# One pool of raw weight tiles for both halves of the MLP, and the first pair's weight forms written earlier

## The chip, the cores and the metric

The kernel runs on one core of a Trainium2 chip. The metric is device time in microseconds (us) for one execution. All engines of the core run their own instruction streams: TensorE (PE, matmuls and transposes, with PEld for its weight loads), VectorE (DVE), ScalarE (ACT), GpSimd (POOL) and SyncE (SP, which here only issues DMAs). They wait for each other on semaphores, and each stream is in order: an instruction that waits holds everything behind it on its engine, and a DMA that waits to be issued holds every later DMA of that queue.

## The reference, cut to what matters

Two layers, 256 tokens of width 2048, float32. Each layer is a mixer (attention and a short gated convolution, both fed by one projection) and an MLP. Cut:

```python
for l in range(DEPTH):                       # 2
    h = _rmsnorm(x, attn_norm_g[l])
    proj = h @ w_in[l]                       # 2048 -> 6144: q, k, v, gate_b, gate_c, conv_in
    attn = differential attention over q, k, v (8 heads), normalised
    conv = gate_b * _short_conv(gate_c * conv_in, conv_w[l])
    x = x + jnp.concatenate([attn, conv], axis=-1) @ w_out[l]
    hm = _rmsnorm(x, mlp_norm_g[l]) @ w_up[l]                  # 2048 -> 8192
    x = x + jnp.square(jax.nn.relu(hm)) @ w_down[l]            # 8192 -> 2048
return x
```

The weights are 2 x (2048 x 6144 + 2048 x 2048 + 2 x 2048 x 8192) float32 numbers, 403 MB, each read once.

## The kernel before

**Numbers in two parts.** TensorE multiplies in a rounded float32 format. Each weight tile is therefore cast to a rounded part (`hi`, on ACT) and a remainder (`lo = raw - hi`, on DVE), and a product is three matmuls (hi x hi, hi x lo, lo x hi; for some products the two activation parts stand side by side, so that two matmuls do). A weight tile of 0.5 MB (128 partitions x 1024 numbers) costs one ACT cast, one DVE subtraction, and then some matmuls. The cast tiles come from a pool `wpool` with three buffers for `hi` and three for `lo`.

**Jobs.** Class `Weights` (L265) holds a list of jobs. `take()` (L310) hands out the next cast tile and sees to it that the casts of the next three jobs (`AHEAD`) are written into the program. A job loads a raw tile by a DMA on SP's queue and casts it in `halves` (L274), or in `column` (L683) for the up weights.

**The mixer** (L599) runs q, k, v for two groups of heads, then the projections gc and ci of the convolution four times (attention of the second group runs between their matmuls), then gb, and last the output projection `o` in four column chunks (`linear`, L325). Its pools, in the order in which they are opened, with their size in each partition: biasp 16 KB, tmp 12 KB (attention's temporaries), rpool 16 KB (four raw tiles of 4 KB), bpool 64 KB (eight tiles of 8 KB: among them the four `cat` tiles that are the input of `o`).

**The MLP** (L667) is made of two passes. In the first, for each of 32 pairs `i` of 128-wide hidden columns, the up projection of the pair is made (`up_part`, L779: two columns c, each in two halves kh of the 2048 inputs), evicted (`evict`, L797), squared with ReLU (`square`, L802, which also writes the activations to DRAM, `hid`, by a DMA on POOL's queue) and, `LAG` = 2 pairs later, multiplied into the left half of the output with a Strassen-like scheme of seven products (`product`, L826). These products need the down weights of pair `i` in several forms, made by `quarters(i)` (L706): b1, b2 straight from the raw tile `draw` (1 MB), t13 and t24 from sums of its quarters, each again as hi and lo. Three jobs make them: `plain` (b1, b2), `sums` (the differences t, and t13) and `more` (t24). For the first pair their ACT and DVE instructions are marked `keep`, that is held in the order in which they are written (`late`, L118). The last two pairs are multiplied without the scheme (L910 to L920, the jobs of `rows`, L741).

In the second pass (L937 to L962) the activations are read back from DRAM (`block`, L884: a load `back` of 0.5 MB and its split into g) and multiplied with the right half of the down weights, one job per 0.5 MB (`weights.straight`, L770), in blocks (b, n) of two jobs each.

**Pools of the MLP.** Opened in this order: fpool 20 KB, dpool 16 KB (two `draw` tiles), and then in a scope `first` spool 40 KB (the weight forms) and upool 24 KB (three raw up tiles `uraw` of 8 KB). `first` is closed after the first pass, and rpool (four raw tiles of 4 KB) and gpool 32 KB are opened in its place. Pools lie on a stack, so a tile of a new pool stands where tiles of the closed pools stood. Its first write waits for the last reader of whatever overlaps it. Mixer and MLP both start at the same address, which gives, in KB of each partition:

```
          0       16     28      44      60      76      92   100  108
mixer     [ biasp  |tmp   |rpool |bpool  0 |  1 |  2 |  3 |  4 |  5 |  6 |  7 ]
MLP, 1st  [ fpool 0-20 | dpool 20-36 | spool 36-76 | upool 76-100 ]
MLP, 2nd  [ fpool 0-20 | dpool 20-36 | rpool 36-52 | gpool 52-84  ]
```

**What sets the order.** PE's instructions run in the order in which they are written. ACT, DVE, POOL and SP are ordered at build time by a scheduler, which places an instruction where its own model thinks it becomes ready, with what is written earlier first. So where a tile lies decides when its load may start, and by that where the load stands in SP's queue.

Of the kernel before, what the change touches and what calls it, by code (L numbers as in the profile page):

```python
# [9 lines left out]
F32 = mybir.dt.float32  # L10
# [5 lines left out]
P = 128  # L16
# [12 lines left out]
CH = 512  # L29
WC = 256  # L30
KG = 4
RAW = 4
# [69 lines left out]
def trunk(ctx: ExitStack, tc: tile.TileContext, x, w_in, w_out, conv_w, q_norm_g, k_norm_g,  # L102
          lambda_q1, lambda_k1, lambda_q2, lambda_k2, subln_g, attn_norm_g, mlp_norm_g,
          w_up, w_down, rel_bias, selector, out):
    nc = tc.nc
# [159 lines left out]
    class Weights:  # L265
# [22 lines left out]
        def plain(self, w, row, c, nk):  # L288

            cols = 2 * CH // nk  # L290

            def make():
                raw = self.early.pop(0) if self.early else load()
                return self.halves(raw)

            def load():
                raw = self.pool.tile([P, nk, cols], F32, tag="raw", name="raw", bufs=RAW)
                nc.sync.dma_start(
                    raw, w[row:row + nk * P, c:c + cols].rearrange("(k p) c -> p k c", p=P))
                return raw  # L300

            make.load = load
            self.jobs.append(make)
# [363 lines left out]
    def mlp(l, mnorm, last):  # L667

        norm = None if last else Norm(0, l + 1)
        mT = mnorm.tiles  # L670
        with ExitStack() as scope:
            fpool = scope.enter_context(tc.tile_pool(name="fpool", bufs=2))
            dpool = scope.enter_context(tc.tile_pool(name="dpool", bufs=2))
            first = scope.enter_context(ExitStack())
            spool = first.enter_context(tc.tile_pool(name="spool", bufs=1))
            upool = first.enter_context(tc.tile_pool(name="upool", bufs=3))
            work.start(mnorm.factors(), 1)


            weights = Weights(None)  # L680
            raws, forms = {}, {}

            def column(i, c, kh):  # L683
# [15 lines left out]
            def load_rows(i, col):  # L699
                raw = dpool.tile([P, 2, 2 * CH], F32, tag="draw", name="draw")  # L700
                nc.sync.dma_start(
                    raw, w_down[l][i * 2 * P:(i + 1) * 2 * P, col:col + 2 * CH].rearrange(
                        "(k p) c -> p k c", p=P))
                return raw

            def quarters(i):  # L706


                keep = late if i == 0 else lambda ins: None

                def parts(src, tag, bufs):
                    hi = spool.tile(list(src.shape), F32R, tag=f"{tag}h", name=f"{tag}h", bufs=bufs)
                    lo = spool.tile(list(src.shape), F32R, tag=f"{tag}l", name=f"{tag}l", bufs=bufs)
                    keep(nc.scalar.activation(hi, src, AF.Copy))  # L714
                    keep(nc.vector.tensor_sub(lo, src, hi.bitcast(F32)))
                    return hi, lo

                def plain():
                    raw = forms["raw"] = load_rows(i, 0).rearrange("p k (n c) -> p k n c", n=2)
                    h1, l1 = parts(raw[:, 0, 0], "b1", 2)  # L720
                    h2, l2 = parts(raw[:, 1], "b2", 1)
                    return (h1, l1), (h2[:, 0], l2[:, 0]), (h2[:, 1], l2[:, 1])

                def sums():
                    raw = forms["raw"]
                    t = forms["t"] = spool.tile([P, 4, CH], F32, tag="t", name="t")

                    keep(nc.vector.tensor_sub(t[:, 0:2], raw[:, :, 1], raw[:, 0]))
                    h, lw = parts(t[:, 0:2], "t13", 1)

                    keep(nc.vector.tensor_add(t[:, 2], t[:, 1], raw[:, 0, 0]))
                    keep(nc.vector.tensor_sub(t[:, 3], raw[:, 1, 0], t[:, 2]))
                    return (h[:, 0], lw[:, 0]), (h[:, 1], lw[:, 1])

                def more():
                    h, lw = parts(forms["t"][:, 2:4], "t24", 1)
                    return (h[:, 0], lw[:, 0]), (h[:, 1], lw[:, 1])

                return plain, sums, more

            def rows(i, k, box):  # L741
# [19 lines left out]
            for i in range(NP - LAG, NP):  # L761
                box = []
# [3 lines left out]


            order = [(b - n, n) for b in range(NB2 + 1) for n in range(2) if 0 <= b - n < NB2]
            for b, n in order:
                weights.straight(w_down[l], b * KG * P, KG, (2 + n) * CH)  # L770


            hid = [dram.tile([P, KG * S], F32, name=f"hid{l}{b}") for b in range(NB2)]
# [23 lines left out]
            def evict(acc, dst):  # L797
                ev = nat.tile([P, 2, S], F32, tag="wide", name="ev")
                nc.scalar.activation(ev, acc, AF.Copy)
                nc.vector.tensor_add(dst.rearrange("p a c -> p (a c)"), ev[:, 0], ev[:, 1])  # L800

            def square(i, h):  # L802


                u = h[:, 0:4].rearrange("p a c -> p (a c)")
                nc.scalar.activation(u, u, AF.Relu)
                top = h[:, 0:4].rearrange("p (k t) c -> p k t c", t=2)[:, :, 0]
                nc.vector.tensor_mul(top, top,
                                     mnorm.ratio.unsqueeze(1).to_broadcast([P, 2, P]))
                nc.scalar.activation(u, u, AF.Square)  # L810
                nc.gpsimd.dma_start(hid[i // 2][:, i % 2 * 2 * S:(i % 2 + 1) * 2 * S], u)  # L811
                n = 4
                if i < NP - LAG:
                    n = 8
                    nc.vector.tensor_add(h[:, S1], h[:, A21], h[:, A22])
                    nc.vector.tensor_sub(h[:, S2], h[:, S1], h[:, A11])
                    nc.vector.tensor_sub(h[:, S3], h[:, A11], h[:, A21])
                    nc.vector.tensor_sub(h[:, S4], h[:, A12], h[:, S2])
                f = fpool.tile([P, 2, 8, P], F32R, tag="f", name="f")
                nc.scalar.activation(f[:, 0, :n], h[:, :n], AF.Copy)  # L820
                nc.vector.tensor_sub(f[:, 1, :n], h[:, :n], f[:, 0, :n].bitcast(F32))
                return f
# [10 lines left out]
            for i in range(NP):  # L833
                j = i - LAG
                end = i == NP - 1
                h = fpool.tile([P, 8, P], F32, tag="h", name="h", bufs=1)
                if i == 0:
                    two = mm.tile([P, 2, CH], F32, tag="mm2", name="up0")
                    two = [two[:, c].rearrange("p (h s) -> p h s", h=2) for c in range(2)]
                    for kh in range(2):  # L840
                        for c in range(2):
                            up_part(two[c], kh)
                            if kh:
                                evict(two[c], h[:, 2 * c:2 * c + 2])
                    fs[0] = square(0, h)
                    continue
                for c in range(2):
                    if i < LAG:
                        acc = bank("upw").rearrange("p (h s) -> p h s", h=2)
                    else:  # L850
                        acc = column_bank()
                    up_part(acc, 0)
                    up_part(acc, 1)
                    evict(acc, h[:, 2 * c:2 * c + 2])
                    if c == 1:
                        fs[i] = square(i, h)
                    if j == 0 and c == 0:
                        for pair in ((1, 6), (2, 3)):
                            w2 = mm.tile([P, 2, CH], F32, tag="mm2", name=f"pr{l}{pair[0]}")
                            prods[pair[0]], prods[pair[1]] = w2[:, 0], w2[:, 1]  # L860
                        for n in (4, 5, 7):
                            prods[n] = bank(f"pr{l}{n}")
                    if j >= 0 and c == 0:
                        b11, b21, b22 = weights.take()
                        t1, t3 = weights.take()
                        product(1, j, A11, b11, end)
                        product(2, j, A12, b21)
                        product(3, j, S4, b22)
                        product(5, j, S1, t1, end)
                        work.tick()  # L870
                    elif j >= 0:
                        t2, t4 = weights.take()
                        product(7, j, S3, t3, end)
                        product(6, j, S2, t2, end)
                        product(4, j, A22, t4)
                        work.tick()


            first.close()
            rpool = scope.enter_context(tc.tile_pool(name="rpool", bufs=RAW))  # L880
            gpool = scope.enter_context(tc.tile_pool(name="gpool", bufs=3))
            weights.pool = rpool

            def block(b):  # L884

# [25 lines left out]
            for j in range(NP - LAG, NP):  # L911
                for k in range(2):
                    b = weights.take()
# [94 lines left out]
```

## Time and profile before

| | |
|---|---|
| median of 3 runs | 2210.66 us (2209.38 to 2211.1) |
| the profiled execution's own time | 2213.11 us, of which the span from first to last instruction is 2211.3 us |
| granted TensorE clock, mean | 0.991 |
| PE busy | 2163.5 us (98%), 11066 matmuls and transposes |
| DVE / ACT / POOL busy | 1610.7 / 1286.7 / 137.8 us |
| read from HBM | 425.84 MB, 201 GB/s over the span |
| one cast of 128x1024 | ACT 1055 ns (L282), DVE 1227 ns (L283) |
| one matmul of 512 columns | starts every 227 ns at full clock |
| loads: `uraw` 1 MB, `draw` 1 MB, `raw` of w_down 0.5 MB, `back` 0.5 MB | 5.7, 5.1, 4.5, 5.3 us from issue to landing (medians) |

How to read it: where an instruction has waited, a row of the timeline ends in the idle time before it and in what ended it. Matmuls are pipelined, so the rows give a matmul of 512 columns about 390 ns while the next one starts 227 ns after it; time lost is read from the starts. PE's granted clock is a share of full speed. The trace names a tile by its name in the program: `uraw`, `uhi`, `ulo` are an up weight tile raw and in its two parts; `draw` is the raw tile of a pair's down weights; `raw`, `whi`, `wlo` are those of all other weights.

### The profile page before, as it was taken

The numbers are of one execution on the slowest core, as the hardware profiler recorded it, in microseconds if no ns is written. First come the engines' busy times: TensorE is split into PE (matmuls) and PEld (weight loads), VectorE is DVE, ScalarE is ACT, GpSimd is POOL, SyncE is SP. The second block draws the span as 40 slices with busy tenths as digits, with TensorE's granted clock in tenths as the row PEclk, the third lists the DMA queues.
The fourth block names the chain that finished last, engine by engine and source line by source line (L and its number), as shares of the span: only waits on it lengthen the run. The fifth ranks groups of instructions, "written<-read, shape, count | busy, mean of one in ns | idle before, by whom it ended". The sixth has DMA issues, their size and how long they took to land.

```text
span 2211.3 us, 29293 instructions
## 1 busy us (share of the span) xinstructions
PE 2163.5 (98%) x11066; PEld 1835.1 (83%) x11066; DVE 1610.7 (73%) x2229; ACT 1286.7 (58%) x1718; POOL 137.8 (6%) x194
## 2 busy tenths in 40 slices
PE   8999999889999999999999999996999999999999
PEld 7888888678888888888888888885888888888887
DVE  6677655589898989755566776555989898987554
ACT  6456445466666666654455654444666666665443
POOL 2021100000000000100011111000000000001000
PEclk9999999999999999999999999998999999999999
DMA  7654666666666666477575546656676666665775
GB/s 260 181 153 153 188 184 180 193 210 207 220 213 214 218 210 217 169 243 242 186 247 174 160 152 189 183 160 211 208 223 208 219 214 213 218 210 198 251 239 161
DMA packets 293518, 446.65 MB, mean 202 GB/s; under 512 B 11427, under 2 KB 192245, under 8 KB 293376
## 3 DMA queue, kind: packets, MB, share of 16 engines
q1 hardware_dynamic: 286672, 423.66, 61.5%
q0 software_dynamic: 6656, 21.10, 2.5%
q8 instruction: 86, 1.41, 0.3%
q14 instruction: 56, 0.46, 0.1%
q10 hardware_dynamic: 48, 0.02, 0.0%
HBM read 425.84 MB, written 18.90 MB: 201 GB/s over the span
## 4 chain that ended last, share of the span: by engine, by line
PE 94%; issue 4%; DMA 1%; DVE 0%; POOL 0%; ACT 0%; SPq 0%; DVEq 0%; POOLq 0%
PE upc L789 30%; PE dn L950 16%; PE pr L829 13%; PE o L338 8%; PE q L338 4%; PE gc L360 4%; PE ci L360 4%; PE gb L360 4%; PE v L338 4%; PE k L338 4%; PE sc L500 1%; PE av L536 1%; DMA hid<-h 1%; DMA raw<-in_w_down_dram 1%; PE tpn L402 1%
## 5 line engine op out<-in xcount | busy, mean ns | idle before, releaser
L283 DVE TENSOR_TENSOR wlo<-raw,whi 128x1024 fp32r<-128x1024 f32 (+1 forms) x386 | 473.4, 1227 | 384.2 <-ACT whi L282 382.8
L282 ACT ACTIVATE whi<-raw 128x1024 fp32r<-128x1024 f32 (+1 forms) x386 | 407.2, 1055 | 481.1 <-PE dn L950 163.6
L789 PE MATMUL upc<-nT,uhi 128*128 128x512 f32 x1920 | 480.2, 392 | 0.0
L694 ACT ACTIVATE uhi<-uraw 128x1024 fp32r<-128x1024 f32 x256 | 270.4, 1057 | 308.2 <-PE upc L789 274.4
L789 PEld LDWEIGHTS upc<-nT,uhi 128*128 128x128 f32 x1920 | 354.9, 189 | 69.0
L695 DVE TENSOR_TENSOR ulo<-uraw,uhi 128x1024 fp32r<-128x1024 f32 x256 | 312.6, 1222 | 121.3 <-ACT uhi L694 118.7
L950 PE MATMUL dn<-whi,g 128*128 128x512 f32 x1024 | 316.3, 389 | 0.0
L789 PEld LDWEIGHTS upc<-nT,ulo 128*128 128x128 f32 x1920 | 262.8, 191 | 18.8
L789 PE MATMUL upc<-nT,ulo 128*128 128x256 f32 x1920 | 268.5, 283 | 0.0
L950 PEld LDWEIGHTS dn<-whi,g 128*128 128x128 f32 x1024 | 192.2, 188 | 40.0
L950 PE MATMUL dn<-wlo,g 128*128 128x512 f32 x512 | 199.2, 389 | 0.0
L338 PE MATMUL o<-whi,cat 128*128 128x512 f32 x512 | 159.6, 390 | 0.0
L338 PEld LDWEIGHTS o<-whi,cat 128*128 128x128 f32 x512 | 96.2, 188 | 19.7
L950 PEld LDWEIGHTS dn<-wlo,g 128*128 128x128 f32 x512 | 96.1, 188 | 19.8
L829 PE MATMUL pr<-t13h,f 128*128 128x512 f32 x240 | 95.1, 396 | 11.5 <-ACT t13h L714 11.5
L338 PE MATMUL o<-wlo,cat 128*128 128x512 f32 x256 | 99.7, 389 | 0.0
L811 POOL DMA_DIRECT2D hid<-h x64 | 34.9, 545 | 982.8 <-ACT h L810 982.8
L338 PE MATMUL q<-whi,nT 128*128 128x512 f32 x256 | 85.7, 404 | 2.7 <-ACT nT L248 2.7
L338 PE MATMUL k<-whi,nT 128*128 128x512 f32 x256 | 85.3, 399 | 0.0
L829 PE MATMUL pr<-t24h,f 128*128 128x512 f32 x240 | 84.0, 390 | 0.0
L829 PE MATMUL pr<-b2h,f 128*128 128x512 f32 x240 | 84.0, 390 | 0.0
L338 PE MATMUL v<-whi,nT 128*128 128x512 f32 x256 | 83.4, 396 | 0.0
(330 smaller groups left out, 3443.5 us busy)
## 6 DMA issues: line engine op xcount, KB each, us to landing
uraw<-in_w_up_dram SPq DMA_DIRECT2D x128, 1024.0 KB, 5.7
raw<-in_w_in_dram SPq DMA_DIRECT2D x192, 512.0 KB, 3.9
draw<-in_w_down_dram SPq DMA_DIRECT2D x64, 1024.0 KB, 5.1
raw<-in_w_down_dram SPq DMA_DIRECT2D x128, 512.0 KB, 4.5
raw<-in_w_out_dram SPq DMA_DIRECT2D x64, 512.0 KB, 3.7
hid<-h POOLq DMA_DIRECT2D x64, 256.0 KB, 3.5
back<-hid SPq DMA_DIRECT2D x32, 512.0 KB, 5.3
rev<-by_dist_d POOLq DMA_DIRECT2D x4, 1024.0 KB, 11.2
```

What stands on the lines that cost most here:

```text
L282: nc.scalar.activation(hi[:, k], raw[:, k], AF.Copy)
L283: nc.vector.tensor_sub(lo[:, k], raw[:, k], hi[:, k].bitcast(F32))
L338: nc.tensor.matmul(acc[:, t], a.ap[:, pa, k % KG, t * P:(t + 1) * P], (hi, lo)[pw][:, j], start=(k == 0 and n == 0), stop=(k == nk - 1 and ...
L360: nc.tensor.matmul(acc[:, f, 0] if part else acc[:, f], wt[:, k % 4, fs], a.ap[:, 0, k % KG] if part else a.ap[:, :, k % KG], start=(part ...
L402: nc.tensor.transpose(tp[:, i * S + t * P:i * S + (t + 1) * P], xs[n][:, t, k * P:(k + 1) * P], ident)
L500: nc.tensor.matmul(sc[:, :W], qT[m * DK:(m + 1) * DK, a, i, t * P:(t + 1) * P], kT[m * DK:(m + 1) * DK, b, i, :W], start=(n == 0), stop=(n ...
L694: nc.scalar.activation(hi, src, AF.Copy)
L695: nc.vector.tensor_sub(lo, src, hi.bitcast(F32))
L789: nc.tensor.matmul(acc[:, 0] if part else acc, wt[:, k], a.ap[:, 0, k % KG] if part else a.ap[:, :, k % KG], start=(part == 0 and kh == 0 ...
L811: nc.gpsimd.dma_start(hid[i // 2][:, i % 2 * 2 * S:(i % 2 + 1) * 2 * S], u)
L829: nc.tensor.matmul(prods[n], fs[j][:, pa, a], b[pw], start=(j == 0 and m == 0), stop=(stop and m == 2))
L950: nc.tensor.matmul(acc[:, t], f[:, pa, k, t * P:(t + 1) * P], (hi, lo)[pw][:, k % 2], start=(b == 0 and k == 0 and m == 0), stop=(b == NB2 ...
```

## The change

It does three things.

1. `upool` becomes the first pool that the MLP opens, and stays open through both passes. The stack of the MLP is then:

```
          0            24        44      60               92   100
MLP, 1st  [ upool 0-24 | fpool 24-44 | dpool 44-60 | spool 60-100 ]
MLP, 2nd  [ upool 0-24 | fpool 24-44 | dpool 44-60 | gpool 60-92 ]
```

2. The second pass has no raw pool of its own. A new helper `four` loads the 1 MB of a block (b, n) with one DMA into a tile of `upool` (same tag `uraw`, so the same three buffers as the up weights) and makes two jobs of it, one per half.

3. For the first pair, `quarters(0)` returns jobs that only hand out forms already made. They are made by `forms["begin"]()`, which is called behind `square(0, h)`: the `draw` load, b1, b2, t and t13 of the first pair are written into the program behind the first pair's up columns, and no longer when the jobs in the list are reached (with the last half column of the second pair and the first of the third). t24 stays where it was.

```diff
         with ExitStack() as scope:
+            upool = scope.enter_context(tc.tile_pool(name="upool", bufs=3))
             fpool = scope.enter_context(tc.tile_pool(name="fpool", bufs=2))
             dpool = scope.enter_context(tc.tile_pool(name="dpool", bufs=2))
             first = scope.enter_context(ExitStack())
             spool = first.enter_context(tc.tile_pool(name="spool", bufs=1))
-            upool = first.enter_context(tc.tile_pool(name="upool", bufs=3))
             work.start(mnorm.factors(), 1)
-            weights = Weights(None)
+            weights = Weights(upool)
...
+                if i == 0:
+                    made = {}
+                    begin = lambda: made.update(p=plain(), s=sums())
+                    forms["begin"] = begin
+                    return lambda: made["p"], lambda: made["s"], more
                 return plain, sums, more
...
             order = [(b - n, n) for b in range(NB2 + 1) for n in range(2) if 0 <= b - n < NB2]
+
+            def four(b, n, k, box):
+                def make():
+                    if k == 0:
+                        raw = upool.tile([P, KG, CH], F32, tag="uraw", name="raw")
+                        nc.sync.dma_start(
+                            raw, w_down[l][b * KG * P:(b + 1) * KG * P,
+                                           (2 + n) * CH:(3 + n) * CH].rearrange(
+                                               "(k p) c -> p k c", p=P))
+                        box.append(raw)
+                    return weights.halves(box[0][:, k:k + 2])
+                weights.jobs.append(make)
+
             for b, n in order:
-                weights.straight(w_down[l], b * KG * P, KG, (2 + n) * CH)
+                box = []
+                four(b, n, 0, box)
+                four(b, n, 2, box)
...
                     fs[0] = square(0, h)
+                    forms["begin"]()
                     continue
...
             first.close()
-            rpool = scope.enter_context(tc.tile_pool(name="rpool", bufs=RAW))
             gpool = scope.enter_context(tc.tile_pool(name="gpool", bufs=3))
-            weights.pool = rpool
```

## The prediction

> **What bounds the kernel now.** First the page's busy times: PE is busy for 2163.5 of 2211.3 us, DVE for 73%, ACT for 58%, so only what makes PE wait, or run slowly, counts. Next PE's list of waits (what waited on what: us in total, times, longest):
>
> ```profile
> PE up L789 <- ACT uhi L694: 18.5, 2, 9.6
> PE pr L829 <- ACT t13h L714: 11.5, 2, 5.8
> PE pr L829 <- DVE t13l L715: 3.1, 2, 2.0
> PE pr L916 <- DVE wlo L283: 1.5, 2, 0.8
> PE up L789 <- ACT ev L799: 1.4, 2, 0.7
> ```
>
> Each stands there twice, once per layer, and all lie around the MLP. The first: TensorE has finished `o` and the first up weights are not cast. Then PE's timeline of layer 0 (start, duration, what, idle before):
>
> ```profile
> 398.03 0.39 PE L338 MATMUL o<-whi,cat 128*128 128x512 f32 x1
> 407.39 3.78 PE L789 MATMUL up<-nT,uhi 128*128 128x512 f32 x8 [8.98 <-ACT uhi L694]
> ...
> 423.11 2.00 PE L789 MATMUL upw<-nT,uhi 128*128 128x512 f32 x8
> ...
> 425.91 2.00 PE L789 MATMUL upw<-nT,uhi 128*128 128x512 f32 x8
> ...
> 447.87 0.79 PE L829 MATMUL pr<-t13h,f 128*128 128x512 f32 x1 [5.76 <-ACT t13h L714]
> 449.76 0.80 PE L829 MATMUL pr<-t13l,f 128*128 128x512 f32 x1 [1.10 <-DVE t13l L715]
> 450.36 0.63 PE L829 MATMUL pr<-t13h,f 128*128 128x512 f32 x1
> 450.78 3.62 PE L789 MATMUL upc<-nT,uhi 128*128 128x512 f32 x8
> ...
> 458.75 0.40 PE L829 MATMUL pr<-t13h,f 128*128 128x512 f32 x1
> ```
>
> A half column takes 425.91 - 423.11 = 2.80 us; eight hi matmuls take 2.00 at full clock and 3.78 behind the gap. So a gap costs more than its length. The clock says why (window, then busy us and count of PE, PEld, DVE, ACT, POOL; granted clock; DMA share; GB/s):
>
> ```profile
> 398.00:400.00 2.00, 0.42 (x2) 0.00 (x0) 1.29 (x2) 0.82 (x3) 0.00 (x0) 1.00 0.96 380
> 402.00:404.00 2.00, 0.00 (x0) 0.00 (x0) 0.55 (x4) 0.00 (x0) 0.00 (x0) 0.50 1.06 336
> 408.00:410.00 2.00, 2.00 (x6) 1.61 (x5) 1.73 (x2) 1.01 (x2) 0.00 (x0) 0.50 0.83 271
> 596.75:612.68 15.93, 15.93 (x86) 13.77 (x86) 14.19 (x20) 10.92 (x14) 0.54 (x1) 1.00 0.70 213
> ```
>
> PE restarts at half clock; in the settled first pass (last line, one pair of columns) it never idles, and DVE is busy 89%. What held the two waits: the up loads are issued only behind the last `o` matmul (398.49), and t13 stands on DVE behind other work and a wait for the `hid` DMA:
>
> ```profile
> 398.49 41.38 SPq L687 DMA_DIRECT2D uraw<-in_w_up_dram  x9
> ...
> 445.51 1.22 DVE L728 TENSOR_TENSOR t<-draw 128x1024 f32<-128x1024 f32 x1
> 448.15 0.42 DVE L800 TENSOR_TENSOR h<-ev 128x256 f32<-128x256 f32 x1 [1.42 <-DMA hid<-h]
> 448.49 1.22 DVE L715 TENSOR_TENSOR t13l<-t,t13h 128x1024 fp32r<-128x1024 f32 x1
> ```
>
> **What can be won.** Stretch A, last `o` matmul to the second pair's first up matmul: 423.11 - 398.03 = 25.1 us, for one `o` matmul (0.23), four half columns (11.2), eight transposes (0.8) and two small matmuls (0.2): 12.4, so 12.7 lost. Stretch B, from there to the second t13 product: 458.75 - 423.11 = 35.6 for eight half columns (22.4) and twelve products (2.7): 25.1, so 10.5 lost. Layer 1, same rows: A 1521.10 - 1495.24 = 25.9, lost 13.4; B 1556.17 - 1521.10 = 35.1, lost 10.0. In all 46.6 us.
>
> **Part 1, upool first.** Before, the `uraw` tiles overlap `cat`, which the last `o` matmul reads. After, they overlap bias and tmp, done with attention. In the order that the scheduler wrote for the changed kernel, three `uraw` loads stand on SP in the mixer, at the second group's end of attention, and wait for its last av matmul (204.0 to 204.8 in the trace); the raw load queued behind two of them was issued at 205.6 anyway, with the cast that frees its tile. They put 3 MB in front of mixer loads. DMA moved 380, 240, 336, 372 and 349 GB/s in the 2 us windows from 398, so the two raw tiles behind 2.5 and 4 MB land at about 213.5 and 217.5; their casts were at 215.5 and 218.3 and the matmuls that need them from 221.9 on. Cover 4 to 7 us: cost 0. The lost time of A is refilled, by rows: uhi of the first half column is cast when `o` frees its buffer, at 392.8, the next at 395.5, the third at 398.45. PE goes on at 398.26. What is late next: (a) the factor matmul rbc. The third cast holds the squares of the norm back by 0.5, and on DVE the fourth ulo (1.2, waiting for the first half column's end, 402.0) now stands ahead of the row factors; with three small operations, two nT of 0.4 and the diagonal, they end at about 404.8, where PE arrives at 404.2: 0.7 (0 to 2). (b) The wait for ev stays: 0.7. (c) nT of the last quarter is just in time: 0.1. A loses 1.5 instead of 12.7 and 13.4.
>
> **Part 3, first forms.** In the new DVE order t and t13l stand ahead of the second pair's h, which waits for the `hid` DMA. The `draw` load moves the other way: it overlaps bpool now and is issued at 398.5 instead of 392.6, behind one uraw load, and lands by about 408; it is needed at 422. From the end of A (411.8) PE reaches the t13l product at 411.8 + 16.8 + 10 x 0.23 = 430.9. DVE, back to back at 1.14 per 1024 and 0.6 per 512 columns, from the ulo that PE releases at 420.4: ulo, f, b1l, b2l, t, h, b1l, ulo, h, ulo, t13l, end 430.5. t24l: DVE 437.5, PE 437.85, if the uraw load issued at 427.75 lands in 5.5 to 6.5, since its cast stands ahead of t24h on ACT. Zero by this count, but by 0.3; I take 0.3, range 0 to 5. DVE's 89% leaves 1.7 us per pair to recover in. So B loses 0.3, and A and B together 1.8 per layer: gain 46.6 - 3.6 = 43.0.
>
> **Part 2, 1 MB loads from upool.** 64 loads of 1 MB for 128 of 0.5 MB: issue time on SP is not on PE's path. A tile now has five jobs of 2.72 us between its release and its next cast (13.6 us) against 5.7 to land, before four jobs (10.9) against 4.5, and PE had no wait there: 0 either way. The change of pools does cost at the seam. Before, DVE made the first three wlo of the pass ahead of the x updates; its rows:
>
> ```profile
> 927.54 3.47 DVE L891 TENSOR_TENSOR g<-back,g 128x1024 fp32r<-128x1024 f32 x1
> 930.93 1.21 DVE L283 TENSOR_TENSOR wlo<-draw,whi 128x1024 fp32r<-128x1024 f32 x1
> ```
>
> Behind these it now has g, wlo, g, x, wlo. The third g needs a `back` load that is issued when the first g ends (931.0). It landed in 3.3 us for the first block, 5.3 is the median: 934.3 to 936.3, then ACT 1.06, g 1.14, x 0.66, wlo 1.2: 938.4 to 940.4. PE needs this wlo at 934.86 + 2.72 + 0.23 = 937.8: 0.6 to 2.6, and the next wlo, behind three x updates, 0.5 more. I take 1.6 per layer, nearer the low end since no raw load stands around this one; 3.2 for two, range 0 to 8. The 0.8 wait on wlo stays: the same g and POOL additions stand before it.
>
> At that seam four loads of the next mixer's w_in now stand on SP behind the last product of the pass (934.9), 1.5 MB ahead of the fourth 1 MB tile, which is needed at about 947 and is there by 944: 0. The next mixer had no wait at its start: 0.
>
> **Sum.** 43.0 - 3.2 = 39.8 us. Against the profiled execution's own 2213.11: 2173.3; that execution is 2.45 above the median of the three runs, so against the median 2170.9, say **2171**. The measurement tells about 0.2% (4.4 us) from no change.
>
> **A rule beside the clock rows.** Rows: 0.7 us of idle (wait for ev) left eight matmuls at 2.12, 9.0 halved the clock. The Trainium skill, "TensorE: Matmul & The Clock Gate" (section "What's actually happening"), puts the limit at an idle window of about 3.4 us, and the same time to be busy before full speed. The trace agrees on both sides of it. By that rule a new wait under 3.4 us costs its length alone, and a longer one about 1.7 more (an estimate from the page); the sum would be the same 2171.
>
> **Rivals.**
> 1. *DVE becomes the bound of the first pairs.* For: t13l and t24l are in time by 0.3 to 0.4 only. Against: DVE's 89%. A late uraw load or `draw` sets PE back by some 5 us per layer, as the 5.76 wait did: 2171 + 10 = 2181.
> 2. *The seam waits for `back`.* If the load takes 8.6 us, as the second did before (925.02 to 933.6), PE idles 6 instead of 1.6 and restarts at half clock (+2): 2171 + 13 = 2184.
> 3. *Slower: the hoisted loads starve the mixer.* They hold SP until attention's last matmul. If the real end came over 15 us behind the scheduler's place (cover 4 to 7 plus 11 for four buffered jobs), gc and ci would wait; it outweighs the gain from 20 us per layer, say 2216. Against: by the trace that matmul ends 0.8 before the next raw tile is free.
> 4. *Nothing changes:* the loads still come late. Only if the pool's first tile waited for `o`; the written order has them in the mixer: 2211.
>
> **Chances.** Forecast 0.70, rival 1 0.14, rival 2 0.09, rival 3 0.04, rival 4 0.03. The forecast's own range is 2165 (all but the ev waits gone, no seam: 2210.7 - 45.2) to 2177 (residues 2 each higher). With the rivals 1 and 2: 2165 to 2185. Faster 0.93, same 0.03, slower 0.04.
>
> **What would show it.** `up <- uhi` and `pr <- t13h` gone from PE's waits; uraw issues near 205 and 1302; granted clock 1.00 at 402; an up matmul at about 398.3; a wait of dn on wlo of 1 to 2 us near 916. Wrong if PE waits on t13l or t24l for over 2 us, or on whi in gc or ci.

## The result, and the profile after

The changed kernel takes 2179.31 us (median of 4 runs, 2178.22 to 2181.14) against 2210.88 before on the same chip: a ratio of 0.9859, 95% interval 0.9841 to 0.9876. That is 31.6 us less. The forecast was 2171, 39.7 less: the sign and four fifths of the size came, and 2179.3 lies 2.3 above the forecast's own range (2165 to 2177), inside the wide one. The profiled execution took 2181.14 us, with a span of 2179.4.

First PE's list of waits in the changed kernel (what waited on what: us in total, times, longest):

```profile
PE up L809 <- ACT ev L819: 3.2, 2, 2.0
PE pr L849 <- DVE f L841: 3.2, 4, 1.0
PE pr L935 <- DVE wlo L283: 1.6, 2, 0.8
PE rbc L436 <- DVE diag L433: 1.1, 2, 0.5
PE dn L969 <- DVE wlo L283: 1.0, 2, 0.6
```

`up <- uhi` (18.5) and `pr <- t13h` (11.5) are gone, as forecast. The waits for `rbc` and `dn <- wlo` were forecast too, and are shorter than forecast. Two are not in the forecast's sum: `up <- ev` has grown from 1.4 to 3.2, and `pr <- f` is new. PE's timeline of layer 0 (start, duration, what, idle before) shows where they lie:

```profile
399.75 0.39 PE L338 MATMUL o<-whi,cat 128*128 128x512 f32 x1
399.97 1.98 PE L809 MATMUL up<-nT,uhi 128*128 128x512 f32 x8
...
406.62 0.46 PE L436 MATMUL rbc<-diag,ones 128*128 128x128 f32 x2 [0.53 <-DVE diag L433]
...
412.32 2.12 PE L809 MATMUL up<-nT,uhi 128*128 128x512 f32 x8 [1.97 <-ACT ev L819]
...
415.22 2.00 PE L809 MATMUL upw<-nT,uhi 128*128 128x512 f32 x8
...
440.29 0.40 PE L849 MATMUL pr<-t13h,f 128*128 128x512 f32 x1
...
441.43 0.50 PE L849 MATMUL pr<-t24l,f 128*128 128x512 f32 x1
...
465.23 0.50 PE L849 MATMUL pr<-b1h,f 128*128 128x512 f32 x1 [0.42 <-DVE f L841]
```

The up matmuls now follow the last `o` matmul 0.22 us later, at full speed. Stretch A is 415.22 - 399.75 = 15.5 us (12.4 needed, 3.1 lost; 14.7 and 2.3 in layer 1). Stretch B is 440.29 - 415.22 = 25.07: the 25.1 that it needs, so nothing is lost. The clock (window, busy us and count of PE, PEld, DVE, ACT, POOL; granted clock; DMA share; GB/s) stays at 1.00 here, over the 1.97 us wait too:

```profile
400.00:402.00 2.00, 2.00 (x11) 1.64 (x10) 1.83 (x3) 1.83 (x4) 0.00 (x0) 1.00 0.51 126
410.00:412.40 2.40, 0.43 (x4) 0.23 (x3) 0.59 (x1) 1.54 (x2) 0.00 (x0) 1.00 1.06 382
```

PE runs the same 11066 matmuls and transposes in the same order in both kernels, so the start of the same matmul in both profiled executions can be subtracted (matched starts, below). That gives the sum term by term:

| stretch | forecast gain, both layers | measured, layer 0 and layer 1 |
|---|---|---|
| start of the program (first q matmuls) | 0 | -1.72 |
| A, last `o` matmul to first `upw` | 23.1 | 9.61 + 11.14 = 20.75 |
| B, to the second t13 product, and t24l | 19.9 | 10.24 + 9.75 = 19.99 |
| products of pairs 2 and 3 (`pr <- f`) | 0 | -2.02 - 2.64 = -4.66 |
| change of pass | -3.2 | -1.23 - 1.06 = -2.29 |
| sum | 39.8 | 32.1 (the spans: 2211.3 - 2179.4 = 31.9) |

### The two new waits, followed back

SP's queue in the changed kernel (start of the first, time to the end of the last, what, how many):

```profile
206.54 0.99 SPq L687 DMA_DIRECT2D uraw<-in_w_up_dram  x2
...
399.80 0.37 SPq L687 DMA_DIRECT2D uraw<-in_w_up_dram  x1
400.34 1.06 SPq L701 DMA_DIRECT2D draw<-in_w_down_dram  x2
405.13 27.99 SPq L687 DMA_DIRECT2D uraw<-in_w_up_dram  x5
...
449.78 0.39 SPq L701 DMA_DIRECT2D draw<-in_w_down_dram  x1
```

The first `uraw` loads stand in the mixer, where the forecast had them (205 expected, 206.5 found), and PE has no wait between 200 and 395. The fourth is issued at 399.80 with two `draw` loads right behind it. ACT's timeline:

```profile
410.72 1.06 ACT L694 ACTIVATE uhi<-uraw 128x1024 fp32r<-128x1024 f32 x1 [3.22 <-DMA uraw<-in_w_up_dram]
411.69 0.58 ACT L819 ACTIVATE ev<-up 128x512 f32<-128x512 f32 x1
...
461.20 0.63 ACT L714 ACTIVATE b1h<-draw 128x512 fp32r<-128x512 f32 x1 [3.85 <-DMA draw<-in_w_down_dram]
461.74 1.04 ACT L714 ACTIVATE t13h<-t 128x1024 fp32r<-128x1024 f32 x1
462.69 1.05 ACT L840 ACTIVATE f<-h 128x1024 fp32r<-128x1024 f32 x1
```

The wait for ev and the first wait for f in each layer have one shape: a cast on ACT waits for a DMA, and something that PE needs stands behind it. At 410.72 it is the cast of the fourth `uraw` tile, with `ev` behind it. At 461.20 it is b1h of pair 3, with the cast of `f` of pair 2 behind it, whose remainder DVE then makes at 463.96, while PE's product began at 464.18. The second wait for f in each layer, at pair 3, comes another way. DVE's rows:

```profile
461.87 0.69 DVE L715 TENSOR_TENSOR b1l<-draw,b1h 128x512 fp32r<-128x512 f32 x1 [2.94 <-ACT b1h L714]
462.82 1.22 DVE L715 TENSOR_TENSOR t13l<-t,t13h 128x1024 fp32r<-128x1024 f32 x1 [0.26 <-ACT t13h L714]
463.96 1.22 DVE L841 TENSOR_TENSOR f<-h,f 128x1024 fp32r<-128x1024 f32 x1
...
481.21 1.22 DVE L841 TENSOR_TENSOR f<-h,f 128x1024 fp32r<-128x1024 f32 x1
```

DVE has stood idle for 3.2 us, for the same late cast, and from 462.82 on it works without a pause until the remainder of pair 3's f is done at 482.4. PE, whose product of pair 3 began at 480.82, waits 1.02 us for it. ACT had cast that f at 478.24, behind no DMA. By matched starts pair 2 loses 0.7 and pair 3 1.3 in layer 0, and 1.3 each in layer 1.

The fourth `uraw` load, asked for alone, took (what, its durations in ns, and us from issue to landing):

```profile
L687 SPq DMA_DIRECT2D uraw<-in_w_up_dram x1: 368/368/368, 399.8 to 399.8; - x1
...
DMA to landing us min/median/max: 10.8/10.8/10.8
```

The median of `uraw` loads was 5.7 us in the kernel before. And the `draw` load of pair 3 is issued when the second of the two `draw` tiles comes free, that is when pair 1's last sum has read it (DVE, 449.07 + 0.68). Before, it was issued at 458.1 and PE reached pair 2's products 18.1 us later than now, at 482.3: 24.2 us. Now it has 464.18 - 449.78 = 14.4, and the load alone takes 11.4, behind an `uraw` load issued 0.6 earlier.

### The profile page after: what moved, and what is told of

The parts are those of the page before. It is cut to its first block, busy times and chain, and to the rows that moved or that the text cites. A ratio compares the mean times of both kernels' runs of the same rounds, so it can differ in the third digit from the quotient of the medians.

```text
span 2179.4 us, 29050 instructions
## 1 busy us (share of the span) xinstructions
PE 2156.6 (99%) x11066; PEld 1828.6 (84%) x11066; DVE 1603.9 (74%) x2229; ACT 1271.7 (58%) x1718; POOL 138.8 (6%) x194
## 4 chain that ended last, share of the span: by engine, by line
PE 94%; DMA 2%; DVE 2%; ACT 1%; issue 1%; SPq 0%; DVEq 0%; ACTq 0%
PE upc L809 29%; PE dn L969 15%; PE pr L849 13%; PE o L338 8%; PE q L338 4%; PE gc L360 4%; PE ci L360 4%; PE k L338 4%; PE gb L360 4%; PE v L338 4%; PE upw L809 1%; DMA uraw<-in_w_up_dram 1%; PE sc L500 1%; PE av L536 1%; PE tpn L402 1%; DMA draw<-in_w_down_dram 1%
## 5 line engine op out<-in xcount | busy, mean ns | idle before, releaser
L969 PEld LDWEIGHTS dn<-whi,g 128*128 128x128 f32 x1024 | 192.2, 188 | 39.7
```

What stands on the lines that cost most here:

```text
L969: nc.tensor.matmul(acc[:, t], f[:, pa, k, t * P:(t + 1) * P], (hi, lo)[pw][:, k % 2], start=(b == 0 and k == 0 and m == 0), stop=(b == NB2 ...
```

## Experiments

Theory from here on: (1) part 1 won A, part 3 won B, independently; part 2 gains nothing. (2) The 7 us that are missing at the first pairs are DMA time: the `draw` loads were moved behind an `uraw` load, and the two `draw` tiles come free too late for a PE that is 18 us earlier. Rival: DVE, or ACT's order, is the bound there, whatever the loads do. All kernels' times stand beside runs of the kernel before on the same chip.

### Part 1 alone

```diff
+            upool = ... # opened first
             fpool = ...
-            upool = ... # opened last
```

> Part 1 alone (upool first; the second pass has its own raw pool and 0.5 MB loads; the first pair's forms made where they were). Theory: stretch A (last o matmul to the second pair's first up matmul) falls from 12.7 and 13.4 us lost to about 3.1 and 2.4, as in the changed kernel, and stretch B keeps its wait on t13 (10.5 and 10.0), since its cause is the place of t13 on DVE behind the second pair's h: 2210.9 - 20.6 = about 2190. Rival: B's wait is set by loads that come at a fixed time, so what A gains B gives back: above 2200. Second rival: B was a consequence of A's late loads and goes with it: below 2182.

Measured 2193.26 against 2211.86 (0.9915, 0.990 to 0.993): 18.6 less. Its list of PE's waits:

```profile
PE pr L842 <- ACT t13h L714: 11.5, 2, 5.8
...
PE up L802 <- ACT ev L812: 3.2, 2, 1.8
```

A's wait for uhi is gone and B's for t13h is the same 11.5 as before; there is no wait for f. Both rivals fall (above 2200, below 2182). It is 3 above the 2190 expected. The wait for ev is here without part 3, so it comes with part 1.

### Part 3 alone

```diff
+                if i == 0:
+                    made = {}
+                    begin = lambda: made.update(p=plain(), s=sums())
+                    forms["begin"] = begin
+                    return lambda: made["p"], lambda: made["s"], more
...
                     fs[0] = square(0, h)
+                    forms["begin"]()
```

> Part 3 alone (before, with the first pair's forms written behind its up columns). Theory: A stays at 12.7 and 13.4, B falls from 10.5 and 10.0 to 1 to 2.5, as in the changed kernel: 2210.9 - 17 = about 2194. Here the draw loads stay in front of the up loads (issued at about 392.6), so no wait of pr on f is expected behind it. Rival: B's loss belongs to the draw or hid transfers and stays: above 2205.

Measured 2197.37 against 2211.86 (0.9933, 0.9916 to 0.9949): 14.5 less, 3 above what was expected. PE's waits:

```profile
PE up L794 <- ACT uhi L694: 17.3, 2, 9.0
...
PE pr L834 <- DVE f L826: 2.0, 2, 1.0
```

A stays, B's wait is gone, and `pr <- f` is there, which was not expected: it does not need the `draw` loads behind an `uraw` load. It comes with part 3, and the tile that frees late is enough for it: in this kernel's trace ACT's cast of pair 3's b1h waits 3.4 us for the `draw` load that was issued at 459.74. PE's wait is at pair 3 alone, once per layer: the one that comes through DVE. The two parts alone gain 18.6 + 14.5 = 33.1, the whole change 31.6 and 32.5 in its two sets of runs: they add up.

### The changed kernel without part 2

The second pass gets its own raw pool and 0.5 MB loads back.

```diff
-                four(b, n, 0, box)
-                four(b, n, 2, box)
+                weights.straight(w_down[l], b * KG * P, KG, (2 + n) * CH)
...
+            rpool = scope.enter_context(tc.tile_pool(name="rpool", bufs=RAW))
```

> Parts 1 and 3 without part 2: the second pass takes its 0.5 MB loads from a pool of its own again. Theory: the loads' size is worth nothing and only the change of pass gains, where the changed kernel waits 0.6 and 0.4 on a wlo in dn: 2178.3 (1 below the changed kernel), no wait of dn on wlo. Rival: the 1 MB loads carry part of the gain: 2183 or more.

Measured 2180.84 (0.9856, 0.9842 to 0.9871), not 2178.3. `dn <- wlo` is down to one wait of 0.2 (none was expected), but its wait for ev was 3.7 in all, with 1.9 in the longer one: in layer 1 ACT waited 3.1 us for the fourth `uraw` load, 2.5 in the changed kernel. And behind that wait PE ran at half clock for 3.4 us (PE's row, then the window's row with the granted clock, 0.50):

```profile
1492.84 3.53 PE L807 MATMUL up<-nT,uhi 128*128 128x512 f32 x8 [1.88 <-ACT ev L817]
...
1494.00:1496.00 2.00, 2.00 (x6) 1.58 (x5) 0.00 (x0) 0.00 (x0) 0.00 (x0) 0.50 0.18 58
```

The eight matmuls take 3.53 here and 2.11 at the same place of the changed kernel. By matched starts stretch A of layer 1 is 2.2 us longer than in the changed kernel, and 0.8 and 1.1 less is lost at the two changes of pass. So the time alone settles nothing on part 2: the load's landing, with the clock behind it, varies by as much as the part is worth. Part 2 is taken out once more below, with that wait out of the way.

### The draw loads in front of the uraw load

```diff
+            dpool = scope.enter_context(tc.tile_pool(name="dpool", bufs=2))
             fpool = scope.enter_context(tc.tile_pool(name="fpool", bufs=2))
-            dpool = scope.enter_context(tc.tile_pool(name="dpool", bufs=2))
```

> The changed kernel with dpool opened before fpool, so that the two draw tiles overlap the mixer's tmp and raw tiles and not cat: the draw loads are issued at about 394 in place of 400.3 and stand in front of the fourth uraw load. Theory: the fourth uraw load (10.9 us to landing, between two draws) lands in about 6, ACT's cast of it no longer holds up ev, and the wait of up on ev falls from 2.0 and 1.25 to 0.7 each: 2177.5, with an uraw to landing of under 7 at 400. Rival: ev is held by ACT's own order (nT, casts), and the waits stay: 2179.3.

Measured 2177.64 (0.9845, 0.983 to 0.9859). The `draw` loads were issued at 393.42, the fourth `uraw` at 398.86. From issue to landing that one took

```profile
DMA to landing us min/median/max: 7.6/7.6/7.6
```

and PE's waits were

```profile
PE pr L849 <- DVE f L841: 2.5, 3, 1.0
...
PE up L809 <- ACT ev L819: 1.4, 2, 0.7
```

The wait for ev is back at the 0.7 of before, although the load took 7.6 and not the 6 expected; the rival (ACT's own order) falls. The waits for f stay. The time alone would not show this gain: its interval overlaps the changed kernel's (0.9841 to 0.9876).

### Three draw tiles, and the changed kernel again

```diff
-            dpool = scope.enter_context(tc.tile_pool(name="dpool", bufs=2))
+            dpools = [... "dpool0", bufs=1 ..., ... "dpool1", bufs=1 ...]   # 24 to 40 KB, ahead of fpool
+            dpools.append(first.enter_context(tc.tile_pool(name="dpool2", bufs=1)))   # 100 to 108 KB
...
-                raw = dpool.tile([P, 2, 2 * CH], F32, tag="draw", name="draw")
+                raw = dpools[i % 3].tile([P, 2, 2 * CH], F32, tag="draw", name="draw")
```

> The changed kernel with three draw tiles in place of two, each in a pool of its own: two at 24 to 40 KB (in front of fpool), the third at 100 to 108 KB. The draw load of pair 3 then no longer waits for the second pair's t24 forms. Theory: this load (issued at 449.8, landed at 461.2) is what holds b1h on ACT, behind it the cast of f and with it pr; issued earlier, it is there in time, and the four waits of pr on f (3.2 us, by matched matmul starts 4.7) go, as well as the long wait for ev: 2179.3 - 4.7 - 1.9 = 2172.7. Rival: f is late because DVE has too much to do in the first pairs: the waits stay, 2177.4, as with dpool in front of fpool alone.

> The changed kernel once more, beside the kernels that are compared with it. 2179.3 by its first runs. If the late start of its first profile (first q matmul at 9.90 us, before 8.63) belongs to the change, it is there again; if it varies from one execution to the next, as the other profiles (8.99 to 9.41) suggest, it lies anywhere between 8.6 and 9.9.

Measured 2173.47 (0.9829, 0.9815 to 0.9844) beside the changed kernel's 2179.04 (0.9855, 0.9838 to 0.9871): 5.6 less, where 6.6 was expected. Pair 3's `draw` load is issued at 435.68 in place of 449.78, and ACT's rows there show no wait for it:

```profile
448.75 0.62 ACT L716 ACTIVATE b1h<-draw 128x512 fp32r<-128x512 f32 x1
...
458.21 1.04 ACT L842 ACTIVATE f<-h 128x1024 fp32r<-128x1024 f32 x1
```

f is cast 4.3 us ahead of PE's product (462.47), where it was 1.5 in the changed kernel (462.69 to 464.18), and PE's list has no `pr <- f` any more; the wait for ev stays at 0.7 each. DVE has the same work as before in these pairs, so the rival, DVE as the bound whatever the loads do, falls. The late load did reach PE through DVE at pair 3, though: here DVE has not lost those 3.2 us, and it ends pair 3's f at 476.6, where PE's product that needs it starts at 478.9. The matched starts of these two kernels put 0.5 of the difference at A in each layer and 1.9 in each layer at the products of pairs 2 and 3.

### The additions of x at the change of pass, on DVE

```diff
-                nc.gpsimd.tensor_tensor(dst, dst, v, op=ALU.add)
+                nc.vector.tensor_add(dst, dst, v)      # written behind the last products
```

> As the kernel with three draw tiles, and the four additions of x at the end of the first pass on DVE in place of POOL. In the trace g<-back takes 3.5 us beside these additions and 1.2 elsewhere. Theory (they slow each other): g takes 1.2, the four additions put 2.6 on DVE in front of it, so the wait of pr on wlo (0.8) stays about as it is, and the wait of dn on wlo (0.6 and 0.4) goes, since the written order has the third g behind two wlo: 1 to 2 below the kernel with three draw tiles, about 2171. Rival: g is slow for another reason (its back tile), stays at 3.5, and the additions come on top: 5 above.

Measured 2169.76 (0.9814, 0.9799 to 0.9829): 3.7 below three draw tiles alone, more than the 1 to 2 expected, and 9.3 below the changed kernel beside it. Here are DVE's rows at the change of pass, first in the changed kernel:

```profile
911.40 3.53 DVE L910 TENSOR_TENSOR g<-back,g 128x1024 fp32r<-128x1024 f32 x1
914.85 1.21 DVE L283 TENSOR_TENSOR wlo<-draw,whi 128x1024 fp32r<-128x1024 f32 x1
915.98 1.21 DVE L910 TENSOR_TENSOR g<-back,g 128x1024 fp32r<-128x1024 f32 x1
917.12 1.21 DVE L283 TENSOR_TENSOR wlo<-raw,whi 128x1024 fp32r<-128x1024 f32 x1
919.35 1.23 DVE L910 TENSOR_TENSOR g<-back,g 128x1024 fp32r<-128x1024 f32 x1 [1.02 <-ACT g L909]
920.49 0.75 DVE L916 SCALAR_TENSOR_TENSOR x<-pr,rowf,x 128x512 f32<-128x512 f32 x1
921.15 1.21 DVE L283 TENSOR_TENSOR wlo<-raw,whi 128x1024 fp32r<-128x1024 f32 x1
```

and with the additions on DVE:

```profile
908.69 1.22 DVE L912 TENSOR_TENSOR g<-back,g 128x1024 fp32r<-128x1024 f32 x1
909.83 1.22 DVE L283 TENSOR_TENSOR wlo<-draw,whi 128x1024 fp32r<-128x1024 f32 x1
910.96 1.22 DVE L912 TENSOR_TENSOR g<-back,g 128x1024 fp32r<-128x1024 f32 x1
912.10 2.35 DVE L283 TENSOR_TENSOR wlo<-raw,whi 128x1024 fp32r<-128x1024 f32 x2
```

The first g takes 1.22 beside an idle POOL and 3.53 beside POOL's additions; both `wlo` waits of PE are gone from its list. In the changed kernel POOL's row for two of them says

```profile
911.26 2.56 POOL L927 TENSOR_TENSOR x<-x,e 128x512 f32<-128x512 f32 x2
```

which ends at 913.82, and g ends 1.1 us after that: it looks blocked until POOL was done, and then took about its usual time. The edit also changes where the additions stand in DVE's order, so how much of the 3.7 comes from g alone was not separated; by matched starts 1.7 and 1.8 of it lie at the two changes of pass. The Trainium skill, "SBUF — State Buffer" (section "Who interferes with whom"), says that a VectorE instruction with two SBUF inputs and a GpSimd instruction that reads SBUF exclude each other for the whole instruction; this case's rows agree.

### Part 2 again, with three draw tiles

```diff
-                four(b, n, 0, box)
-                four(b, n, 2, box)
+                weights.straight(w_down[l], b * KG * P, KG, (2 + n) * CH)
...
+            rpool = scope.enter_context(tc.tile_pool(name="rpool", bufs=RAW))
```

> The kernel with three draw tiles, but with the second pass's 0.5 MB loads from a pool of its own, as before the change (parts 1 and 3 without part 2, free of the varying wait for ev). Theory: part 2 gains nothing in the steady second pass and costs at the change of pass, where g stands between the first wlo: by matched matmul starts 0.8 and 1.1 less lost there, so 1.8 below the kernel with three draw tiles, 2171.7, and no wait of dn on wlo over 0.4. Rival: 1 MB loads are worth something elsewhere: the same as the kernel with three draw tiles, 2173.5, or above it.

> The kernel with three draw tiles once more, beside the one with 0.5 MB loads: 2173.5 by its first runs, with 0.6 us waits of dn on wlo at each change of pass.

Measured 2171.72 (2170.63 to 2173.12) with 0.5 MB loads, 2173.37 (2172.14 to 2174.81) with 1 MB. 1.65 less, and the two sets of runs overlap a little. What the times alone leave open, the traces place: by matched starts the two differ by more than 0.3 only at the start of the program and at the two changes of pass (0.7 and 1.2 less lost). PE's wait there with 0.5 MB loads:

```profile
PE dn L971 <- DVE wlo L283: 0.3, 1, 0.3
```

With 1 MB loads it is 1.2 in two waits. The kernel without part 2 above gave 0.8 and 1.1 there. So part 2 costs about 1 us per layer and gives nothing back that these runs can see.

## Why the prediction was right, and where it fell short

**Part 1, the place of the loads: right.** The three loads in the mixer cost nothing, PE goes on behind `o` without a gap, and the half clock behind the old gaps went with them. Part 1 alone gave 18.6 of it. (The prediction's rule on the clock was that a new wait under 3.4 us costs its length alone. It held in the changed kernel, where no wait behind the program's start is longer than 1.97 us and the clock stays at 1.00. It did not hold in the kernel without part 2: there a wait of 1.88 us was followed by 3.4 us at half clock, which cost about 1.5 us on top, since stretch A was 2.2 longer and the wait only 0.6. So the length of one wait does not decide alone. In the 3.41 us before that drop PE was busy for 45%; what decides stays open.)

**Part 1, what is late next: the term (b) was mis-sized.** rbc cost 0.5 (0.7 forecast). The wait for ev was to stay at 0.7 and was 2.0 and 1.25; A came 2.4 us short in the two layers. The step that failed is in part 3's paragraph: it noted that the `draw` loads move behind one `uraw` load, and asked only when they land, not what they do to the load in front. (They land at 413.2 and 415.7, not by 408, and still ahead of their use.) With two loads of 1 MB behind it, that load took 10.8 and 10.1 us in the two layers (10.0 and 10.0 in the second profile of the same kernel); with one behind it, in the kernel with three tiles, 8.2 and 8.7; with none, 7.6 and 7.7. Moved in front, the wait was 0.7 again.

**Part 3, B: right.** 19.99 against 19.9, t24l at 0.2 late (0.3 forecast), t13 in time.

**Part 3, the pairs behind: missing from the sum.** 4.66 us were lost at the products of pairs 2 and 3, for which the sum had nothing. The count of DVE's work ended with the first pair's forms. It did not ask when the *next* `draw` tile comes free, now that PE reaches its product 18 us sooner: the old stall had covered that load. Rival 1 had named a late `draw` load as a trigger, at 5 us per layer and 0.14; it came, at 2.0 and 2.6 per layer. At pair 2 it came through ACT, where the cast of f stands behind a cast that waits for the load. At pair 3 it came through DVE, as rival 1 had it. The prediction left DVE 1.7 us per pair to recover in; against 3.2 us of idle that leaves 1.5 (an estimate from these two numbers), and PE lost 1.3. DVE is in time without the late load, as the third tile shows. At t13l and t24l, where rival 1 saw the narrow margin, nothing came of it.

**Part 2: right in sign, and smaller.** 2.3 lost at the changes of pass against 3.2; the third g did come ahead of the wlo that PE needed, by the mechanism named. Its load was there by 918.2, that wlo was ready 4.1 us later, and PE had waited 0.57 for it (1.6 forecast). Rivals 2, 3 and 4 did not come. The median of 2179.3 is nearer to rival 1's 2181 than to the forecast's 2171: both of its triggers, a late `uraw` and a late `draw` load, came, and cost about 3.5 us per layer together, where it had 5.

**The rest.** 1.7 of the difference between the two profiles lies in the first 50 us and is not the change's: the first q matmul started at 8.63 us before and 9.90 after, and at 7.77 in the second profile of the changed kernel. The account of the two profiles is 23.1 - 20.75 = 2.4 at A, 4.66 at f, 1.7 at the start, less 0.9 at the change of pass: 7.8 of the 39.8. What stays open: the profiled execution of before is 2.2 above its median, with an early start, and no trace of a faster execution of that kernel is at hand to say where those 2.2 lie.

## What to carry to other kernels

When a stall in front of an engine is removed, list for every load behind it how much time it had and how much it has now: the stall was cover for the next buffers to come free, and the queue that frees them did not get faster. A load that is moved to stand directly behind another one is a cost to the one in front as well; move it to where the queue is idle, or give it a buffer that is free by then. And where an in-order engine casts what a DMA brings, look at what stands behind that cast: that is what the other engine will be seen to wait for. An engine that is busy for 89% catches up slowly: here 3.2 us of idle on DVE were still felt one pair later.

## What the runs showed of the hardware that was not expected

- The load in front is not done when it would be alone. Of the fourth `uraw` load's 1024 packets of 1 KB, 999 had ended by 406.0, 6.2 us behind its issue; the last ones came later, among the `draw` loads' packets of 4 KB, and the load had landed at 410.6. The trace does not name the DMA engine of a packet, so why some lagged stays open; that the loads behind it matter is shown by 10.0 to 10.8 us with two, 8.1 to 8.9 with one (over all profiles of kernels with three tiles) and 7.6 to 7.7 with none. The Trainium skill, "DMA: Bandwidth & Descriptors" (section "Queues, rings and completion order"), says that each DMA engine takes descriptors in the order of its ring and that completion is not first-in-first-out per issuing engine; no run here shows a single ring.
- A DVE subtraction of 128x1024 takes 3.5 us in place of 1.2 while POOL adds; the forecast took that row as the price of g, where moving the additions away gained 3.7 us of the whole time.
- The first q matmul of the program started anywhere from 7.66 to 9.90 us in eleven profiled executions of kernels that do not differ there. Each time it was nT on ACT, behind a cast that waited for the first weight load. This spread of 2.2 us is of the size of that between the runs of one kernel (2178.2 to 2181.1), and a comparison of two single profiles has to leave it out.
- A wait of 1.88 us was followed by half clock for 3.4 us (the kernel without part 2, layer 1), while waits of 1.97 us (changed kernel) and 1.80 us (the same kernel, layer 0) were not. It is the only drop behind so short a wait in the eleven profiles.
